# A filter's last layer and first DFT stage in parts of TensorE's array, and full end pieces in attention

## The chip, the cores and the metric

The kernel runs on one core of a Trainium2 chip. TensorE (PE in the profile) multiplies a stationary operand of up to 128x128 with a moving one and writes to PSUM; VectorE (DVE), ScalarE (ACT) and GpSimd (POOL) do the rest, SyncE (SP) issues the transfers. The metric is the device time of one execution in microseconds.

## The reference

An encoder layer is applied to two sequences, A (1024 tokens) and B (512 tokens), with the same weights. Two branches work on the same normalised input: a long convolution with a filter that a small network generates, and attention in three dilated groups. Gates, an output projection and an MLP follow. The parts that the change touches:

```python
def implicit_filter(L, w1, b1, w2, b2, w3, b3, freq, w_out):
    ...
    h = jnp.sin(fr * (h @ w3.astype(f32) + b3.astype(f32)))
    h = h @ w_out.astype(f32)
    ...
    decay = jnp.exp(-t * deltas[None, :])
    h_fwd, h_bwd = jnp.split(h, 2, axis=-1)
    h_fwd, h_bwd = h_fwd * decay, h_bwd * decay
    k2 = jnp.concatenate([h_fwd, jnp.zeros((1, D_HYENA), f32), h_bwd[1:][::-1]], axis=0)
    return k2 / jnp.sum(jnp.abs(k2), axis=0, keepdims=True)

def long_conv(u, k2, d):
    ...
    K = jnp.fft.rfft(k2, n=2 * L, axis=0)
    y = jnp.fft.irfft(U * K[None], n=2 * L, axis=1)[:, :L]
    return (y + uf * d.astype(jnp.float32)).astype(u.dtype)

def banded_attention(q, k, v, bias_vec, radius):
    ...
    p = jnp.exp(s - m)
    den = jnp.sum(p, axis=-1, keepdims=True)
    o = jnp.einsum('...bqk,...bkd->...bqd', p, vw.astype(jnp.float32)) / den
```

The filter has 64 hidden units and 768 channels, forward and backward; the radius of each attention group is 64 keys on each side (in the group's dilated order).

## The kernel before

**The main stream.** All large projections go through one helper, `mm3` (its matmul is L756). Weights and activations are split into a high and a low part, and three products are summed: 128x128 weights, 512 tokens moving. There are 9504 such matmuls. The units of work (18 for the convolution's inputs, 18 for queries, keys and values, 16 gates, the mixing, the output and the MLP, for A and then B) run in a fixed list; names like `zhyA__mm` or `qkvA__mm` tell the unit's kind and group.

**The side work.** Filters, convolutions, attention, norms and gates are generators that yield a cost and a latency at each step, in microseconds. While a unit emits its products, `pump` advances a clock by their cost and, in proportion, resumes side generators that are ready. So the costs that a generator yields set which side work is written between which products. ACT runs in the order in which the program is written; for PE, DVE, POOL and SP the framework's scheduler orders the instructions when the program is built, and each engine then works strictly through its list.

**The filter** (`filt_gen`, `filt_third`). Taps are handled in blocks of 128: 64 forward taps and 64 backward taps. A has 16 blocks, B has 8. The hidden layer's values for a block are a stationary 128x128 tile of `sall`, block-diagonal: 64 hidden units by 64 forward taps above, 64 by 64 backward taps below, zeros elsewhere, which a memset on POOL writes once. The channels are taken in thirds of 256. For each third and each group of four blocks (`jg`), `taps` multiplies that tile with the output weights `fwo` (L835, two blocks into one PSUM bank by `pss2`), DVE multiplies by the decay (L837), ACT takes absolute values (L840) and POOL adds them up (L841) for the norm, which L858 sums over partitions. `stage1` is the first DFT stage: the constant 128x128 tile `f1k` (in `csq`) times the taps (L848), copied out by ACT (L376, the helper `copy`) and stored. `f1k` has nonzero values only in two 64x64 quarters, from forward rows to one half of the outputs for two of the four `q`, and from the backward rows. `stage2` follows with 128x128 constants (L878).

Each step of `taps` and `stage1` handles two blocks and then yields 0.9. Small products take their PSUM from a ring of four banks (`pss`); the main stream has a ring of its own.

**Attention** (`att_gen`). A chain handles 128 queries (or two times 128): scores (L1216, 64 rows of the array for each of two heads, into two banks), scale and bias and maximum on DVE (L1222, L1225), exponentials on ACT (L1232), transposes of the probabilities (L1242), copies by ACT, and P·V (L1256), where the two head pairs write partitions 0 to 63 and 64 to 127. The window of keys is split at multiples of 128, so each chain has two pieces: in the middle both have 128 keys; at the ends, and in half of the windows of group 1, one has 64. Then transposes give 64 rows, a copy is made for each piece, and P·V takes 64 rows of the array for one piece and 128 for the other. Eight chains have such a piece (six in A, two in B).

Of the kernel before, what the change touches and what calls it, by code (L numbers as in the profile page):

```python
# [13 lines left out]
AF = mybir.ActivationFunctionType  # L14
# [47 lines left out]

def _filter_consts(L):
# [15 lines left out]

    decay = decay.reshape(J // 4, 4, 128, 3, 256).transpose(3, 0, 2, 1, 4)  # L80
# [3 lines left out]
def _dft_consts():  # L84
# [10 lines left out]
    f1k = np.zeros((2, 4, 16, 4, 32))  # L95
# [230 lines left out]
def _program(ctx, tc, d, outs):  # L326
# [435 lines left out]
    def filt_gen(S):  # L762
# [7 lines left out]
        sall = g((J // 2, 128)), g((J // 2, 128))  # L770
        for s in sall:
            G_.memset(s, 0.0)
# [24 lines left out]
        for ck in range(2):  # L797
            A.activation(sall[ck][0:64, :, 0:64], arg[64 * ck:64 * ck + 64].rearrange("p (j c) -> p j c", c=64), AF.Sin)
        yield 0.0, 1.0
        for j in range(J):  # L800
            dst = sall[j // nj][64:128, j % nj, 64:128]
# [13 lines left out]
    def filt_third(S, th, sall, fwo):  # L815
# [9 lines left out]
        def taps(jg):  # L825
# [4 lines left out]
            k2[jg] = kt  # L830
            for jp in range(2):
                ps = pss2()
                for jj in range(2):
                    j = 4 * jg + 2 * jp + jj
                    T.matmul(ps[:, jj], sall[j // (J // 2)][:, j % (J // 2), :], fwo[:, cs], start=True, stop=True)  # L835
                sl = slice(2 * jp, 2 * jp + 2)
                V.tensor_tensor(kt[:, sl], ps, dec[:, sl], ALU.mult)  # L837
# [3 lines left out]
                G_.tensor_tensor(acc, acc, ab, ALU.add)  # L841

        def stage1(jg):
            st = g((4, 256))
            for jp in range(2):
                ps = pss2()
                for jj in range(2):
                    T.matmul(ps[:, jj], f1k, k2[jg][:, 2 * jp + jj], start=True, stop=True)  # L848
                copy(st[:, 2 * jp:2 * jp + 2], ps)
                yield 0.9, 0.0  # L850
# [287 lines left out]
    def v_unit(S, gi, f, ratio):  # L1138
# [44 lines left out]
    def att_gen(S, gi):  # L1183
# [11 lines left out]
        def keys(i):  # L1195
# [6 lines left out]
            return k0, k1, [(t0 - k0, min(n, k1 - t0), vv) for t0, n, vv in vts if k0 <= t0 < k1]  # L1202


        def chain(tiles):
# [6 lines left out]
            s = [sp.tile([128, 512 // w, w], F32, tag="sc", name=nm("sc"), bufs=4) for _ in range(2)]  # L1212
            for a, f, i in slots:
# [22 lines left out]
            for hh in range(2):  # L1236
                pt = pss().rearrange("p (a b) -> p a b", a=4)
                pT.append(sp.tile([128, 4, 128], F32, tag="pT", name=nm("pT"), bufs=4))
                pieces = k[tiles[0]][2]
                for a, f, i in slots:  # L1240
                    for j, (o, n, _) in enumerate(k[i][2]):
                        T.transpose(pt[:n, a * np_ + j], s[hh][:, a, o:o + n], ident)  # L1242
                na = len(slots) * np_
                if all(n == 128 for _, n, _ in pieces):
                    copy(pT[hh][:, :na], pt[:, :na])
                else:
                    for j, (o, n, _) in enumerate(pieces):
                        copy(pT[hh][:n, j:na:np_], pt[:n, j:na:np_])
            yield 0.22 * np_ * len(slots), LPT
            po = pss().rearrange("p (a b) -> p a b", a=4)  # L1250
            for b, i in enumerate(tiles):
                for hh in range(2):
                    for j, (o, n, vv) in enumerate(k[i][2]):
                        for f in range(2):
                            h = 2 * f + hh
                            T.matmul(po[64 * f:64 * f + 64, 2 * b + hh], vv[:n, 64 * h:64 * h + 64],  # L1256
                                     pT[hh][:n, (2 * b + f) * np_ + j], start=j == 0, stop=j == np_ - 1)
# [471 lines left out]
```

## Time and profile before

| | |
|---|---|
| median of 3 runs | 2676.79 us (2670.54 to 2680.43) |
| profiled execution | 2664.77 us, its span 2663.0 us |
| PE busy | 2591.3 us (97%) |
| DVE, ACT, POOL busy | 1253.4, 863.9, 153.2 us |
| mean granted clock of TensorE | 0.990 |
| last layer and first DFT stage (L835, L848) | 288 instructions on PE |
| P·V of attention (L1256) | 448 instructions on PE, 64 of them on 64 rows |

In the groups of instructions a row names line, engine, operation, result and operands, then the rows and columns of the array that are used (128*32 is 128 rows and 32 columns), the moving operand (128x256) and the count; after the bar stand busy time, mean duration in ns, and idle time ahead with its cause. In a timeline a row gives start, duration, engine and the same names. A matmul's duration runs to the end of its pass through the array, and the next one starts before that; so what one costs is read from the distance of starts.

### The profile page before, as it was taken

The numbers are of one execution on the slowest core, as the hardware profiler recorded it, in microseconds if no ns is written. First come the engines' busy times: TensorE is split into PE (matmuls) and PEld (weight loads), VectorE is DVE, ScalarE is ACT, GpSimd is POOL, SyncE is SP. The second block draws the span as 40 slices with busy tenths as digits, with TensorE's granted clock in tenths as the row PEclk, the third lists the DMA queues.
The fourth block names the chain that finished last, engine by engine and source line by source line (L and its number), as shares of the span: only waits on it lengthen the run. The fifth ranks groups of instructions, "written<-read, shape, count | busy, mean of one in ns | idle before, by whom it ended". The sixth has DMA issues, their size and how long they took to land.

```text
span 2663.0 us, 30782 instructions
## 1 busy us (share of the span) xinstructions
PE 2591.3 (97%) x12296; PEld 2096.3 (79%) x12296; DVE 1253.4 (47%) x1626; ACT 863.9 (32%) x1414; POOL 153.2 (6%) x108
## 2 busy tenths in 40 slices
PE   8999999999899999999799999999999999999999
PEld 4778888687688777878578877888888888888887
DVE  5354444554658544554455464333333333554544
ACT  5443232533423444443333342112111221322332
POOL 0110100000001211000022210000000000000000
PEclk9999999999999999999899999999999999999999
DMA  7354455565756443446763532111111111422222
GB/s 270 126 165 158 155 165 174 154 187 143 220 204 227 145 135 96 150 153 220 223 202 130 189 126 69 50 48 48 48 48 55 49 43 54 149 101 91 102 95 103
DMA packets 138101, 350.98 MB, mean 132 GB/s; under 512 B 19016, under 2 KB 50303, under 8 KB 137830
## 3 DMA queue, kind: packets, MB, share of 16 engines
q1 hardware_dynamic: 137670, 348.22, 40.1%
q8 instruction: 97, 1.59, 0.3%
q0 software_dynamic: 288, 0.79, 0.1%
q14 instruction: 46, 0.38, 0.0%
HBM read 280.67 MB, written 71.16 MB: 132 GB/s over the span
## 4 chain that ended last, share of the span: by engine, by line
PE 86%; DVE 5%; DMA 4%; ACT 2%; issue 1%; SPq 1%; POOL 1%; DVEq 0%; ACTq 0%; POOLq 0%
PE ffA__mm L756 26%; PE ffB__mm L756 13%; PE zhyA__mm L756 7%; PE qkvA__mm L756 6%; PE mixA__mm L756 6%; PE gateA__mm L756 5%; PE zhyB__mm L756 4%; PE qkvB__mm L756 3%; PE mixB__mm L756 2%; PE gateB__mm L756 2%; PE convA__s L999 1%; DMA mixA__g<-zhyA__dr 1%; PE convA__s L974 1%; PE attA__s L1256 1%; PE filtA__s L878 1%
## 5 line engine op out<-in xcount | busy, mean ns | idle before, releaser
L756 PE MATMUL ffA__mm<-ffA__g,ffA__wh 128*128 128x512 f32 x1024 | 274.1, 389 | 0.0
L756 PE MATMUL ffA__mm<-normA__g,ffA__wh 128*128 128x512 f32 x992 | 265.1, 389 | 0.0
L756 PEld LDWEIGHTS ffA__mm<-ffA__g,ffA__wh 128*128 128x128 f32 x1024 | 192.0, 188 | 40.5 <-issue 0.4
L756 PEld LDWEIGHTS ffA__mm<-normA__g,ffA__wh 128*128 128x128 f32 x992 | 186.2, 188 | 38.7
L1507 DVE SCALAR_TENSOR_TENSOR mixA__g<-ffA__mm,adam,mixA__g 128x1024 f32<-128x1024 f32 x64 | 82.1, 1283 | 190.0 <-PE ffA__mm L756 190.0
L756 PE MATMUL ffB__mm<-ffB__g,ffB__wh 128*128 128x512 f32 x512 | 157.8, 389 | 0.0
L756 PE MATMUL ffA__mm<-ffA__g,ffA__wl 128*128 128x512 f32 x512 | 157.6, 389 | 0.0
L756 PE MATMUL zhyA__mm<-init__g,zhyA__wh 128*128 128x512 f32 x512 | 150.8, 410 | 3.1 <-DVE zhyA__g L1023 3.1
L756 PE MATMUL ffB__mm<-normB__g,ffB__wh 128*128 128x512 f32 x496 | 152.7, 389 | 0.0
L756 PE MATMUL ffA__mm<-normA__g,ffA__wl 128*128 128x512 f32 x496 | 152.7, 389 | 0.0
L389 ACT CAST ffA__wh<-ffA__wr 128x1024 fp32r<-128x1024 f32 x63 | 66.3, 1053 | 256.6 <-PE ffA__mm L756 213.6
L1489 DVE SCALAR_TENSOR_TENSOR ffA__g<-ffA__mm,ffA__g 128x1024 f32<-128x1024 f32 x32 | 39.2, 1225 | 222.4 <-ACT ffA__g L1488 222.4
L756 PE MATMUL gateA__mm<-init__g,gateA__wh 128*128 128x512 f32 x480 | 132.1, 394 | 5.1 <-ACT gateA__wh L389 5.1
L756 PE MATMUL qkvA__mm<-init__g,qkvA__wh 128*128 128x512 f32 x416 | 119.1, 402 | 0.0
L756 PE MATMUL mixA__mm<-mixA__g,mixA__wh 128*128 128x512 f32 x424 | 115.4, 392 | 3.7 <-DVE mixA__g L1441 2.0
L756 PEld LDWEIGHTS zhyA__mm<-init__g,zhyA__wh 128*128 128x128 f32 x512 | 94.4, 189 | 23.9 <-issue 6.4
L756 PEld LDWEIGHTS ffB__mm<-ffB__g,ffB__wh 128*128 128x128 f32 x512 | 96.0, 188 | 20.3 <-ACT ffB__g L389 0.2
L756 PEld LDWEIGHTS ffA__mm<-ffA__g,ffA__wl 128*128 128x128 f32 x512 | 96.1, 188 | 20.0
L1488 ACT ACTIVATE ffA__g<-ffA__mm 128x1024 f32<-128x1024 f32 x32 | 33.0, 1030 | 237.3 <-PE ffA__mm L756 237.3
L756 PEld LDWEIGHTS gateA__mm<-init__g,gateA__wh 128*128 128x128 f32 x480 | 90.0, 189 | 24.1 <-ACT gateA__wh L389 5.3
L756 PEld LDWEIGHTS ffB__mm<-normB__g,ffB__wh 128*128 128x128 f32 x496 | 93.1, 188 | 19.4
L756 PEld LDWEIGHTS ffA__mm<-normA__g,ffA__wl 128*128 128x128 f32 x496 | 93.1, 188 | 19.3
(495 smaller groups left out, 5013.4 us busy)
## 6 DMA issues: line engine op xcount, KB each, us to landing
ada__g<-ada SPq DMA_DIRECT2D x32, 512.0 KB, 4.3
ffA__wr<-w_up SPq DMA_DIRECT2D x32, 512.0 KB, 3.1
ffA__wr<-w_dn SPq DMA_DIRECT2D x32, 512.0 KB
ffB__wr<-w_dn SPq DMA_DIRECT2D x32, 512.0 KB
ffB__wr<-w_up SPq DMA_DIRECT2D x30, 512.0 KB, 3.2
filtA__dr<-filtA__g SPq DMA_DIRECT2D x24, 512.0 KB, 3.6
convA__g<-filtA__dr SPq DMA_DIRECT2D x48, 256.0 KB, 6.2
init__g<-ada SPq DMA_DIRECT2D x16, 512.0 KB, 10.5
```

What stands on the lines that cost most here:

```text
L389: A.copy(hi, raw)
L756: T.matmul(ps[:, 512 * c:512 * c + 512], ww[:, sl], xx(k)[:, 512 * c:512 * c + 512], start=k == 0 and p == 0, stop=k == kt - 1 and p == 2)
L878: T.matmul(ps[:, ee], cm[:, e], sin[:, e], start=True, stop=True)
L974: T.matmul(ps[:, ee], cb_[:, 2 * ep + ee], y[:, 2 * ep + ee], start=True, stop=True)
L999: T.matmul(ps[:, :, 4 * j8:4 * j8 + 4], bt[j // 4][:, j % 4, 128 * cc:128 * cc + 128], ibm, start=True, stop=True)
L1256: T.matmul(po[64 * f:64 * f + 64, 2 * b + hh], vv[:n, 64 * h:64 * h + 64], pT[hh][:n, (2 * b + f) * np_ + j], start=j == 0, stop=j == np_ - 1)
L1488: A.activation(r, ps[:, :L], AF.Relu)
L1489: V.scalar_tensor_tensor(r, ps[:, :L], 0.0, r, ALU.max, ALU.mult)
L1507: V.scalar_tensor_tensor(S.h(m), ps[:, :L], mod(S, 5, m), S.h(m), ALU.mult, ALU.add)
```

## The change

**Filter.** `sall` holds only the two 64x64 quarters, side by side as [128, 16 blocks, 64], so that no zeros are stored or multiplied. A block's product is four parts: 64 hidden units by 32 taps each, on 64 rows and 32 columns of the array. `TAPS` says which quarter of the taps goes to which 32 columns. It alternates the row halves along the columns and differs between the first and the second pair of blocks in a group, so that two blocks, one from each pair, use all eight 64x32 parts of the array, each block writing its own bank. The decay's rows are permuted in the same way. `f1k` becomes two 64x128 halves with a copy for either arrangement, and the DFT stage does two blocks at once in four 64x64 parts. Both steps now handle all four blocks of a group and yield 1.3 once, instead of 0.9 twice.

**Attention.** A piece of 64 keys is filled to 128: the missing rows of `vo` are set to zero, the scores' tile gets zero columns past the window (a memset on POOL for each tile of scores), transposes and P·V always have 128 rows, and one copy takes all pieces.

```diff
+TAPS = ((0, 3, 1, 2), (2, 1, 3, 0))
...
+    piece = decay.reshape(J, 4, 32, DH)
+    decay = np.stack([piece[j, list(TAPS[j % 4 // 2])] for j in range(J)]).reshape(J, 128, DH)
...
-            f1k[0, q, :, q, r] = col(p[:16], r)
-            f1k[1, 3 - q, :, q, r] = col(31 - p[:16], r)
+            if q < 2:
+                for h in range(2):
+                    for s in range(2):
+                        f1k[h, s, q, :, s, q, r] = col(p[:16], r)
+                        f1k[h, 1 - s, 1 - q, :, s, q, r] = col(31 - p[:16], r)
...
-        sall = g((J // 2, 128)), g((J // 2, 128))
-        for s in sall:
-            G_.memset(s, 0.0)
+        sall = g((J, 64))
+        G_.memset(sall[64:128, 0], 0.0)
...
+            ps = pss2(), pss2()
+            for jj in range(2):
+                for jp in range(2):
+                    for i, c in enumerate(TAPS[jp]):
+                        rs = slice(64 * (c // 2), 64 * (c // 2) + 64)
+                        T.matmul(ps[jp][32 * i:32 * i + 32, jj], sall[rs, 4 * jg + 2 * jp + jj, 32 * (c % 2):32 * (c % 2) + 32],
+                                 fwo[rs, cs], start=True, stop=True)
             for jp in range(2):
-                ps = pss2()
-                for jj in range(2):
-                    j = 4 * jg + 2 * jp + jj
-                    T.matmul(ps[:, jj], sall[j // (J // 2)][:, j % (J // 2), :], fwo[:, cs], start=True, stop=True)
                 sl = slice(2 * jp, 2 * jp + 2)
-                V.tensor_tensor(kt[:, sl], ps, dec[:, sl], ALU.mult)
-                yield 0.9, LTAP
+                V.tensor_tensor(kt[:, sl], ps[jp], dec[:, sl], ALU.mult)
+            yield 1.3, LTAP
...
             st = g((4, 256))
+            ps = pss2(), pss2()
+            for jj in range(2):
+                for jp in range(2):
+                    for h in range(2):
+                        o = 64 * (h ^ jp)
+                        T.matmul(ps[jp][o:o + 64, jj], f1k[64 * h:64 * h + 64, 64 * jp:64 * jp + 64],
+                                 k2[jg][64 * h:64 * h + 64, 2 * jp + jj], start=True, stop=True)
             for jp in range(2):
-                ps = pss2()
-                for jj in range(2):
-                    T.matmul(ps[:, jj], f1k, k2[jg][:, 2 * jp + jj], start=True, stop=True)
-                copy(st[:, 2 * jp:2 * jp + 2], ps)
-                yield 0.9, 0.0
+                copy(st[:, 2 * jp:2 * jp + 2], ps[jp])
+            yield 1.3, 0.0
...
+                            if n < 128:
+                                G_.memset(vo[n:, o + a_], 0.0)
...
+            pieces = k[tiles[0]][2]
+            full = max(o for o, _, _ in pieces) + 128
+            for t in s if full > nk else ():
+                G_.memset(t[:, :, nk:full], 0.0)
...
-                        T.transpose(pt[:n, a * np_ + j], s[hh][:, a, o:o + n], ident)
+                        T.transpose(pt[:, a * np_ + j], s[hh][:, a, o:o + 128], ident)
                 na = len(slots) * np_
-                if all(n == 128 for _, n, _ in pieces):
-                    copy(pT[hh][:, :na], pt[:, :na])
-                else:
-                    for j, (o, n, _) in enumerate(pieces):
-                        copy(pT[hh][:n, j:na:np_], pt[:n, j:na:np_])
+                copy(pT[hh][:, :na], pt[:, :na])
...
-                            T.matmul(po[64 * f:64 * f + 64, 2 * b + hh], vv[:n, 64 * h:64 * h + 64],
-                                     pT[hh][:n, (2 * b + f) * np_ + j], start=j == 0, stop=j == np_ - 1)
+                            T.matmul(po[64 * f:64 * f + 64, 2 * b + hh], vv[:, 64 * h:64 * h + 64],
+                                     pT[hh][:, (2 * b + f) * np_ + j], start=j == 0, stop=j == np_ - 1)
```

Since the steps yield other costs, side work stands at other places in the engines' lists, and since the lines shift, the changed kernel's numbers differ: `mm3` is L768, taps L848, the first DFT stage L867, the norm's sum L879, scores L1243, transposes L1268, P·V L1278. In the rows that follow, the number behind "x" at the end is a count, and the shape is that of the result in PSUM.

TensorE at the first group of taps of A's filter, before:

```order
L756 MATMUL qkvA__mm_750<-init__g_255,qkvA__wl_661 128x512 x2
L835 MATMUL filtA__s_764<-filtA__g_447,filtA__g_449 128x256 x2
L756 MATMUL qkvA__mm_750<-init__g_316,qkvA__wh_660 128x512 x2
L756 MATMUL qkvA__mm_750<-init__g_320,qkvA__wh_660 128x512 x2
L756 MATMUL qkvA__mm_750<-init__g_316,qkvA__wl_661 128x512 x2
L650 MATMUL qkvA__s_774<-qkvA__g_654,csq 32x256 x4
L650 MATMUL qkvA__s_774<-qkvA__g_740,csq 32x256 x4
L835 MATMUL filtA__s_789<-filtA__g_447,filtA__g_449 128x256 x2
```

and now:

```order
L848 MATMUL filtA__s_762<-filtA__g_447,filtA__g_449 32x256 x4
L848 MATMUL filtA__s_763<-filtA__g_447,filtA__g_449 32x256 x4
L848 MATMUL filtA__s_762<-filtA__g_447,filtA__g_449 32x256 x4
L848 MATMUL filtA__s_763<-filtA__g_447,filtA__g_449 32x256 x4
L662 MATMUL qkvA__s_782<-qkvA__g_652,csq 32x256 x4
L662 MATMUL qkvA__s_782<-qkvA__g_738,csq 32x256 x4
L768 MATMUL qkvA__mm_748<-init__g_316,qkvA__wh_658 128x512 x2
```

Two steps of two matmuls, with six products of the main stream between them, have become one step of 16, which writes two banks (762 and 763) in turn.

TensorE at the first DFT stage of A's last third, before:

```order
L848 MATMUL filtA__s_2300<-filtA__g_2272,csq 128x256 x2
L848 MATMUL filtA__s_2304<-filtA__g_2272,csq 128x256 x2
L858 MATMUL filtA__s_2309<-filtA__g_2070,csq 128x256 x2
L848 MATMUL filtA__s_2318<-filtA__g_2153,csq 128x256 x2
L848 MATMUL filtA__s_2322<-filtA__g_2153,csq 128x256 x2
L848 MATMUL filtA__s_2328<-filtA__g_2213,csq 128x256 x2
```

and now:

```order
L867 MATMUL filtA__s_2347<-filtA__g_2313,csq 64x256 x3
L867 MATMUL filtA__s_2348<-filtA__g_2313,csq 64x256 x2
L867 MATMUL filtA__s_2347<-filtA__g_2313,csq 64x256
L867 MATMUL filtA__s_2348<-filtA__g_2313,csq 64x256 x2
L879 MATMUL filtA__s_2360<-filtA__g_2105,csq 128x256 x2
L867 MATMUL filtA__s_2369<-filtA__g_2195,csq 64x256 x2
L867 MATMUL filtA__s_2370<-filtA__g_2195,csq 64x256 x2
L867 MATMUL filtA__s_2369<-filtA__g_2195,csq 64x256 x2
L867 MATMUL filtA__s_2370<-filtA__g_2195,csq 64x256 x2
```

The stage stands at the same place, with eight matmuls for a group of four blocks instead of four.

TensorE after an attention chain of A's group 0, with taps of the filter's second third, now:

```order
L1278 MATMUL attA__s_1379<-attA__pT_1341,qkvA__g_1133 64x128 x4
L848 MATMUL filtA__s_1391<-filtA__g_447,filtA__g_449 32x256 x4
L848 MATMUL filtA__s_1392<-filtA__g_447,filtA__g_449 32x256 x4
L848 MATMUL filtA__s_1391<-filtA__g_447,filtA__g_449 32x256 x4
L848 MATMUL filtA__s_1392<-filtA__g_447,filtA__g_449 32x256 x4
L1243 MATMUL attA__s_1411<-qkvA__g_840,qkvA__g_465 128x256
L1243 MATMUL attA__s_1412<-qkvA__g_840,qkvA__g_465 128x256
L1243 MATMUL attA__s_1411<-qkvA__g_853,qkvA__g_502 128x256
L1243 MATMUL attA__s_1412<-qkvA__g_853,qkvA__g_502 128x256
```

Here the taps' two banks are followed at once by scores into two more; before, six products of the main stream stood on each side of two of the taps' matmuls.

More of the change, by code (lines that the diff above doesn't have):

```diff
@@ L797, in filt_gen @@
         for ck in range(2):
[L798 removed]
+            A.activation(sall[0:64, nj * ck:nj * ck + nj],
+                         arg[64 * ck:64 * ck + 64].rearrange("p (j c) -> p j c", c=64), AF.Sin)
         yield 0.0, 1.0
         for j in range(J):
[L801 removed]
+            dst = sall[64:128, j]
             q0 = Q - 4 * j - 3
@@ L844, in stage1 @@
             st = g((4, 256))
-            for jp in range(2):
-                ps = pss2()
-                for jj in range(2):
-                    T.matmul(ps[:, jj], f1k, k2[jg][:, 2 * jp + jj], start=True, stop=True)
-                copy(st[:, 2 * jp:2 * jp + 2], ps)
-                yield 0.9, 0.0
+            ps = pss2(), pss2()
+            for jj in range(2):
+                for jp in range(2):
+                    for h in range(2):
+                        o = 64 * (h ^ jp)
+                        T.matmul(ps[jp][o:o + 64, jj], f1k[64 * h:64 * h + 64, 64 * jp:64 * jp + 64],
+                                 k2[jg][64 * h:64 * h + 64, 2 * jp + jj], start=True, stop=True)
+            for jp in range(2):
+                copy(st[:, 2 * jp:2 * jp + 2], ps[jp])
+            yield 1.3, 0.0
             del k2[jg]
@@ L1201, in keys @@
                 k1 = min(k0 + per, n0 + 192)
-            return k0, k1, [(t0 - k0, min(n, k1 - t0), vv) for t0, n, vv in vts if k0 <= t0 < k1]
+            return k0, k1, [(t0 - k0, n if n < 128 else min(n, k1 - t0), vv) for t0, n, vv in vts if k0 <= t0 < k1]
         def chain(tiles):
@@ L1238, in chain @@
                 pT.append(sp.tile([128, 4, 128], F32, tag="pT", name=nm("pT"), bufs=4))
-                pieces = k[tiles[0]][2]
                 for a, f, i in slots:
-                    for j, (o, n, _) in enumerate(k[i][2]):
-                        T.transpose(pt[:n, a * np_ + j], s[hh][:, a, o:o + n], ident)
+                    for j, (o, _, _) in enumerate(k[i][2]):
+                        T.transpose(pt[:, a * np_ + j], s[hh][:, a, o:o + 128], ident)
                 na = len(slots) * np_
-                if all(n == 128 for _, n, _ in pieces):
-                    copy(pT[hh][:, :na], pt[:, :na])
-                else:
-                    for j, (o, n, _) in enumerate(pieces):
-                        copy(pT[hh][:n, j:na:np_], pt[:n, j:na:np_])
+                copy(pT[hh][:, :na], pt[:, :na])
             yield 0.22 * np_ * len(slots), LPT
@@ L1252, in chain @@
                 for hh in range(2):
-                    for j, (o, n, vv) in enumerate(k[i][2]):
+                    for j, (_, _, vv) in enumerate(k[i][2]):
                         for f in range(2):
                             h = 2 * f + hh
-                            T.matmul(po[64 * f:64 * f + 64, 2 * b + hh], vv[:n, 64 * h:64 * h + 64],
-                                     pT[hh][:n, (2 * b + f) * np_ + j], start=j == 0, stop=j == np_ - 1)
+                            T.matmul(po[64 * f:64 * f + 64, 2 * b + hh], vv[:, 64 * h:64 * h + 64],
+                                     pT[hh][:, (2 * b + f) * np_ + j], start=j == 0, stop=j == np_ - 1)
             for b, i in enumerate(tiles):
```

3 lines of the change are left out of this document (2 added, 1 removed).

## The prediction

> **What bounds the kernel now.** I read the engines' busy times first, then the chain that ended last, then the stretches in which the filter runs.
>
> ```profile
> span 2663.0 us, 30782 instructions
> PE 2591.3 (97%) x12296; PEld 2096.3 (79%) x12296; DVE 1253.4 (47%) x1626; ACT 863.9 (32%) x1414; POOL 153.2 (6%) x108
> ...
> PE 86%; DVE 5%; DMA 4%; ACT 2%; issue 1%; SPq 1%; POOL 1%; DVEq 0%; ACTq 0%; POOLq 0%
> ```
>
> TensorE is busy for 97% of the span, and 86% of the chain is its work. But an average over stages does not say whether it binds where the change is made. Group A's filter and its first attention groups run from 84 to 310 us, group B's filter from 929 to 1200 us:
>
> ```profile
> 84.00:310.00 226.00, 224.43 (x1161) 182.13 (x1160) 101.08 (x140) 91.41 (x202) 33.20 (x26) 1.00 0.43 141
> 310.00:930.00 620.00, 595.90 (x3043) 482.02 (x3043) 341.82 (x549) 217.67 (x426) 28.54 (x22) 0.98 0.58 181
> 929.00:1200.00 271.00, 268.66 (x1408) 214.90 (x1407) 140.19 (x227) 125.92 (x281) 21.14 (x16) 1.00 0.42 133
> 1200.00:1330.00 130.00, 113.27 (x492) 91.33 (x491) 53.96 (x67) 40.97 (x55) 2.39 (x1) 0.93 0.69 220
> ```
>
> The columns after the stretch's length are the busy times of PE, its weight loads, DVE, ACT and POOL. In the two filter stretches PE lacks 1.6 of 226 us and 2.3 of 271 us, at a granted clock of 1.00. Side work there always finds a large product of the main stream beside it. So in these stretches a microsecond of PE work less should be a microsecond of time less. In the other two PE lacks 24.1 and 16.7 us: there it waits for transfers, and there the gain could be lost or enlarged.
>
> **The filter's products.** A program's fp32 matmul is two instructions in the profile, which I call passes.
>
> ```profile
> L835 PE MATMUL filtA__s<-filtA__g,filtA__g 128*128 128x256 f32 x96 | 24.6, 380 | 0.0
> L848 PE MATMUL filtA__s<-filtA__g,csq 128*128 128x256 f32 x96 | 22.7, 379 | 0.0
> L835 PE MATMUL filtB__s<-filtB__g,filtB__g 128*128 128x256 f32 x48 | 12.6, 380 | 0.0
> L848 PE MATMUL filtB__s<-filtB__g,csq 128*128 128x256 f32 x48 | 11.9, 381 | 0.0
> ```
>
> The 380 ns are one pass from its start to its end; passes overlap, so the price is the distance of starts, which the chain shows:
>
> ```profile
> 104.58 1.73 PE filtA__s L835 x8
> 302.06 5.18 PE filtA__s L848 x24
> 749.60 58.29 PE gateA__mm L756 x256
> ```
>
> 1.73/8 and 5.18/24 are both 0.216 us per pass of 256 columns; a pass of the main stream (512 columns) costs 58.29/256 = 0.228 us. Last layer (L835) and first DFT stage (L848) together are 288 passes, 62.2 us of PE. Per group of four blocks each is 8 passes, 1.73 us. There are 12 such groups for A (four times three thirds) and 6 for B.
>
> The change turns the 8 passes of the last layer into 32 (16 matmuls of 64x32), those of the stage into 16 (8 of 64x64). Whether that is cheaper depends only on how many run at once. The trace has the case of four column strips, twice, and that of two row halves:
>
> ```profile
> 94.49 0.62 PE L756 MATMUL qkvA__mm<-init__g,qkvA__wl 128*128 128x512 f32 x2
> 95.04 1.07 PE L650 MATMUL qkvA__s<-qkvA__g,csq 128*32 128x256 f32 x16
> 96.04 1.13 PE L835 MATMUL filtA__s<-filtA__g,filtA__g 128*128 128x256 f32 x4
> ...
> 901.38 0.64 PE L1071 MATMUL qkvB__s<-qkvB__g,csq 128*32 128x128 f32 x16
> 901.95 0.66 PE L1320 MATMUL combineA__s<-csq,combineA__g 128*128 128x128 f32 x4
> ...
> 716.20 1.16 PE L1216 MATMUL attA__s<-qkvA__g,qkvA__g 64*128 64x128 f32 x16
> 717.29 0.50 PE L756 MATMUL gateA__mm<-init__g,gateA__wl 128*128 128x512 f32 x1
> 717.63 0.39 PE L756 MATMUL gateA__mm<-init__g,gateA__wh 128*128 128x512 f32 x1
> ```
>
> L650's 16 passes take 96.04 - 95.04 = 1.00 us. One after the other they would take 16 x 0.216 = 3.46 us, four at a time 0.86 us, so four do run at once. L1071 puts 16 passes into 0.57 us, 36 ns each with their weight loads, so issuing eight in 0.216 us (27 ns each) is near what has been done. L1216 puts 16 passes of two row halves into 1.09 us, where a pass of 128 columns takes half of 0.216: two at a time.
>
> So I take eight 64x32 parts, or four 64x64 parts, per 0.216 us. A group of four blocks is then four rounds in both stages, 0.86 instead of 1.73 us. Saved: 18 groups x 2 stages x 0.865 = **31.1 us**. No row has eight at once. The bound from below is four at once, L650's number: the last layer then needs eight rounds, 1.73 us as before, and half of the 31.1 us, 15.6 us, is gone. From above nothing is faster than the passes of one strip, so 31.1 us is the most.
>
> **Going in and out.** Between the two main-stream passes at 94.49 us and L650 lie 0.55 us instead of 2 x 0.228: 0.10 us. L650's 1.00 us hold 0.14 us beyond the four rounds. The first full pass after such a visit takes 717.63 - 717.29 = 0.34 instead of 0.228 us: 0.11 us. So a visit costs 0.35 us, 0.175 us for each change of array shape. In TensorE's order I count 142 changes of shape before and 186 after (those inside attention's P·V left out, which come next): the 36 stage groups make 33 visits, while side work that now stands together saves some. 44 x 0.175 = **7.7 us lost**; with L1216's visit (0.22 beyond its eight rounds, the same 0.10 and 0.11) 9.5 us, with L650's inner and following parts alone (0.25 us a visit) 5.5 us.
>
> **Attention's end pieces.** P·V of a chain with an end piece, and of one without:
>
> ```profile
> 160.45 1.54 PE L1256 MATMUL attA__s<-attA__pT,qkvA__g 64*64 64x128 f32 x16
> 161.92 1.09 PE L1242 MATMUL attA__s<-csq,attA__sc 128*128 128x128 f32 x8
> ...
> 179.31 1.09 PE L1256 MATMUL attA__s<-attA__pT,qkvA__g 128*64 128x128 f32 x16
> 180.33 1.09 PE L1242 MATMUL attA__s<-csq,attA__sc 128*128 128x128 f32 x8
> ```
>
> The same 16 passes take 1.47 us where 64-row and 128-row pieces alternate and 1.02 us where they do not. Full pieces take 0.45 us off each of 8 such chains (two ends and four half windows in A, two ends in B): **3.6 us gained**, at most this and at least nothing. The transposes keep their number. The fills are 12 memsets of 128x2x64 and 4 of 64x256 on POOL, 6% busy, while the two large ones for the filter shrink. Some stand ahead of the filter's sums in POOL's queue, and PE's L858 waits for those sums; but these memsets wait only for transposes that stand earlier in PE's order than the taps whose sums are behind them.
>
> ```profile
> L819 POOL MEMSET filtA__g<- 128x512 f32 x3 | 1.6, 525 | 85.7 <-DMA filtA__dr<-filtA__g 34.9 <-DVE zhyA__g L1028 26.1 <-PE bias__s L1354 24.7
> ```
>
> Uncovered, 16 at 0.53 us (the time of a larger one) would be 8 us; I take 0, since POOL is idle.
>
> **New waits.** A group of taps now holds two of the four small PSUM banks until DVE has multiplied both, and both become ready together:
>
> ```profile
> L837 DVE TENSOR_TENSOR filtA__g<-filtA__s,filtA__g x24: 679/690/692, 94.3 to 297.3; 128x512 f32<-128x512 f32 x24
> L376 ACT COPY filtA__g<-filtA__s x24: 587/587/590, 125.8 to 307.3; 128x512 f32<-128x512 f32 x24
> ...
> PE filtA__s L858 <- POOL filtA__g L841: 1.4, 1, 1.4
> ```
>
> Where scores or transposes follow taps at once (at three places in the order), they want two banks more, or four, and wait up to 2 x 0.69 = 1.4 us. Where three stage groups stand in a row (at two places), PE needs 0.86 us a group and ACT 2 x 0.587 = 1.17 us, where before PE's 1.73 us hid the copies: the third group waits 2 x (1.17 - 0.86) = 0.6 us. The wait of L858 (1.4 us) stays. Queued behind each wait is the main stream, as PE works in order. Together up to 5.4 us; I take **4 us lost**, between 0 and 9, since other groups stand only a few passes from such work.
>
> **Sum:** -31.1 + 7.7 - 3.6 + 4 = -23.0 us. The profiled execution took 2664.8 us (span 2663.0), which becomes 2641.8. The runs shown have the median 2676.8, 12 us above it; the same difference gives **2654 us**.
>
> **Rivals.** *Four parts at once in the last layer.* For it speaks that no row shows more; against it, L1071's 36 ns per pass. Gain 15.6 us less: 2669 us.
>
> *The gain is given back later.* PE's idle 24.1 and 16.7 us come from convolution stages that wait for transfers. The filter now ends some 100 main-stream passes earlier in the order (740 against 846 before its last product), so convolutions start beside other units. I give this 8 us in either direction, a fifth of the 41 us of idle time. With the largest waits and dearest visits (-31.1 + 9.5 - 3.6 + 9 + 8) it leaves -8 us: 2669 us.
>
> *Slower: two row halves cannot write one bank together.* L1216's two halves write two banks, and L650's four strips write one bank from the same rows; in the change each block's bank gets strips from both halves. If a part must wait for the other half's part in its bank, and all behind it wait too, the parts go one by one: per group 32 x 0.216 = 6.91 instead of 1.73 us in the last layer and 16 x 0.216 = 3.46 in the stage, 18 x (5.18 + 1.73) = 124 us lost, with the other terms +133 us: 2809 us. If the halves only swap banks between rounds, both stages cost what they did, and the other terms give +8 us: 2685 us. It decides from the point where fewer than four 64x32 or two 64x64 parts run at once. Against it: strips lie on different partitions of the bank.
>
> The Trainium skill has a rule of this kind ("TensorEngine Tiling (Array Packing)", Restrictions and Gotchas): row tiles write to different PSUM banks and cannot use the same one at a time. No run here shows it yet; by it one of the last two times would hold. Against it stands "TensorE: Matmul & The Clock Gate", Part 3, with 16 tiles of 32x32 measured at 10.6 times one, by which my sum stays; it lays each row on its own bank, and the trace shows no more than four.
>
> **How the numbers follow.** The forecast 0.66; four at once 0.08; gain given back 0.10; banks 0.12 (of that 0.05 one by one); 0.04 for anything else. The forecast's own range is 2640 (cheap visits, no waits, 8 us gained later: -37.2) to 2669 us. With part of the bank rival I take 2638 to 2680 us. About 0.5%, 13.4 us, is what a measurement of this kernel tells from no change. Faster by more: nearly all of the forecast and a quarter of the two middling rivals, 0.68. Slower: one by one, some of the rest, 0.10. Within: 0.22.
>
> **What would show it.** Right: the filter's stages at about 0.86 us per group plus 0.35 us per visit in the timeline of PE; P·V of end chains at 1.02 us; the stretch up to the filter's end shorter by some 15 us for A and 8 for B; PE's idle time about 4 us longer there. Wrong: groups of taps at 1.73 us (four at once, or swapped banks) or 7 us (one by one), or short groups with PE idle longer by the same amount beyond 310 us.

## The result, and the profile after

| | before | after |
|---|---|---|
| median of 5 runs each, compared | 2676.79 us (2668.58 to 2681.09) | 2627.52 us (2624.71 to 2631.51) |
| profiled execution | 2664.77 us, span 2663.0 us | 2630.32 us, span 2628.5 us |
| ratio | | 0.9838 (95% interval 0.9819 to 0.9857) |

The change is 1.6% faster, 38 to 48 us by the interval. The prediction was 2654 us with a range from 2638 us: the sign was right, the size was not, and the time lies below the range.

Of the page after, the span and the busy times:

```profile
span 2628.5 us, 31915 instructions
PE 2562.4 (97%) x12872; PEld 2061.4 (78%) x12872; DVE 1248.1 (47%) x1626; ACT 860.8 (33%) x1398; POOL 152.0 (6%) x122
```

PE was without work for 2663.0 - 2591.3 = 71.7 us before and for 66.1 us now. The prediction had made PE wait longer, not shorter. The same four stretches as in the prediction (columns: PE, weight loads, DVE, ACT, POOL, granted clock, share of DMA, GB/s):

```profile
84.00:310.00 226.00, 221.35 (x1595) 169.34 (x1595) 106.70 (x149) 90.61 (x201) 33.24 (x32) 1.00 0.52 167
310.00:930.00 620.00, 601.00 (x3185) 486.99 (x3185) 349.25 (x558) 232.56 (x445) 35.58 (x34) 0.98 0.57 176
929.00:1200.00 271.00, 271.00 (x1589) 214.76 (x1589) 142.81 (x235) 118.77 (x260) 14.92 (x13) 1.00 0.51 161
1200.00:1330.00 130.00, 113.97 (x491) 92.37 (x491) 55.77 (x68) 44.01 (x59) 7.19 (x3) 0.91 0.68 214
```

In A's filter (84 to 310 us) PE now lacks 4.7 us where it lacked 1.6: new waits of the filter are there, 3.1 us. Elsewhere it lacks less: 19.0 for 24.1 us, 0.0 for 2.3 us (B's filter), 16.0 for 16.7 us. The 4 us of the forecast were for both filters, which together lack less than 1 us more.

The filter's products themselves, first in PE's timeline at the first group of taps (start, duration, then as before):

```profile
93.13 0.61 PE L768 MATMUL qkvA__mm<-init__g,qkvA__wl 128*128 128x512 f32 x2
93.67 1.09 PE L848 MATMUL filtA__s<-filtA__g,filtA__g 64*32 64x256 f32 x32
94.69 1.07 PE L662 MATMUL qkvA__s<-qkvA__g,csq 128*32 128x256 f32 x16
95.70 0.50 PE L768 MATMUL qkvA__mm<-init__g,qkvA__wh 128*128 128x512 f32 x1
...
122.72 1.13 PE L879 MATMUL filtA__s<-filtA__g,csq 128*128 128x256 f32 x4 [1.60 <-POOL filtA__g L858]
123.79 1.94 PE L867 MATMUL filtA__s<-filtA__g,csq 64*64 64x256 f32 x22
125.97 1.94 PE L867 MATMUL filtA__s<-filtA__g,csq 64*64 64x256 f32 x26 [0.25 <-DVE filtA__g L883]
127.84 0.50 PE L768 MATMUL qkvA__mm<-init__g,qkvA__wh 128*128 128x512 f32 x1
...
161.32 1.97 PE L1278 MATMUL attA__s<-attA__pT,qkvA__g 128*64 128x128 f32 x32
163.22 1.09 PE L848 MATMUL filtA__s<-filtA__g,filtA__g 64*32 64x256 f32 x32
164.24 1.13 PE L1243 MATMUL attA__s<-qkvA__g,qkvA__g 64*128 64x256 f32 x8
```

32 passes of taps take 94.69 - 93.67 = 1.02 us with what it costs to change shape, so eight parts do run at once: in the trace of the single passes eight start within 46 ns, the next eight from 240 ns on, and the 32 starts span 0.72 us. The 16 passes of a single stage group, four parts at once, take 1.02 us as well (the one from 193.4 us on). Two chains of P·V take 163.22 - 161.32 = 1.90 us, 0.95 each. Where three stage groups stand in a row, they take 127.84 - 123.79 = 4.05 us for 3 x 0.86 = 2.59 us of passes.

The waits of PE, longest in total first (total us, times, longest), of before:

```profile
PE init__s L698 <- ACT init__g L696: 9.3, 8, 7.1
PE convB__s L963 <- DMA convB__g<-convB__dr: 8.4, 2, 7.5
PE gateA__mm L756 <- ACT gateA__wh L389: 5.1, 1, 5.1
...
PE zhyA__mm L756 <- DVE zhyA__g L1023: 3.1, 1, 3.1
```

and after:

```profile
PE init__s L710 <- ACT init__g L708: 10.1, 8, 7.6
PE convB__s L1020 <- DMA convB__g<-convB__dr: 8.8, 1, 8.8
PE gateA__mm L768 <- ACT gateA__wh L401: 7.5, 1, 7.5
...
PE filtA__s L879 <- POOL filtA__g L858: 3.5, 3, 1.7
```

No single wait carries the gain: the three largest have grown, the norm's sum (L879) has grown from 1.4 to 3.5 us, and one of before (`zhyA__mm` for L1023) is gone, which comes up again below.

**Where the time went.** I took the starts of all PE passes from 25 us on and sorted what lies between successive starts: passes at their full rate (by the distances of the prediction: 0.216 us for 256 columns, a quarter of it each where four run at once, an eighth for eight); what is beyond that at a change of array shape, up to 0.24 us each; what is beyond it elsewhere (waits); and all of the excess, waits or slow passes, that lies in a stretch where the granted clock is one half. The last 376 us, an unbroken main stream alike in all kernels, are left out. The last two rows are kernels of the experiments below.

| us, one profiled execution each | passes | changes of shape | waits | excess at half clock | (time at half clock) |
|---|---|---|---|---|---|
| before | 2124.5 | 31.0 | 46.4 | 60.3 | 51 |
| before, profiled again | 2124.5 | 30.8 | 45.5 | 72.2 | 75 |
| the change | 2093.5 | 38.5 | 38.8 | 56.7 | 51 |
| whole products in the change's steps | 2124.5 | 22.1 | 33.7 | 54.8 | 48 |
| the change, yield 2.3 | 2093.5 | 48.3 | 45.9 | 75.4 | 85 |

Between the two profiles that is -31.0 us for passes, +7.5 for shapes, -7.6 for waits, -3.6 at half clock. The sorting is not firm in every column. The column of passes is a count at the prediction's prices. In three rows the excess at half clock is more than the time at half clock, so it holds waits from outside these stretches; if only gaps that touch such a stretch are counted, it goes from 40.3 us before to 44.3 us, and waits go from 65.1 to 51.1 us. The sum of the two is firm: 106.7 to 95.5 us by the table, 105.4 to 95.4 us by the other count.

When the two kernels are compared by the start of the same main-stream product, they are level at product 1152 (432 us), although A's filter, over by then in both, has 24 x 0.865 = 20.8 us of passes less. Of the convolution 6.1 us of passes have moved ahead of that point; the other 14.7 us are eaten by more excess, by the second count 5.2 us at changes of shape and 9.5 us in waits. From there to product 1536, in A's convolution, the passes cost the same (143.3 and 142.8 us), yet the change needs 154.5 us where before needs 173.8. So the gain shows at product 1536 (18.5 us), and then at 1920 (24.4 us) and 4224 (35.8 us).

### The profile page after: what moved, and what is told of

It reads as the page before. It is cut to its first block, busy times and chain, and to the rows that moved or that the text cites. A ratio compares the mean times of both kernels' runs of the same rounds, so it can differ in the third digit from the quotient of the medians.

```text
span 2628.5 us, 31915 instructions
## 1 busy us (share of the span) xinstructions
PE 2562.4 (97%) x12872; PEld 2061.4 (78%) x12872; DVE 1248.1 (47%) x1626; ACT 860.8 (33%) x1398; POOL 152.0 (6%) x122
## 4 chain that ended last, share of the span: by engine, by line
PE 50%; DVE 1%; DMA 1%; ACT 0%; issue 0%; SPq 0%; DVEq 0%; ACTq 0%
PE ffA__mm L768 27%; PE ffB__mm L768 13%; PE mixA__mm L768 6%; PE mixB__mm L768 2%; PE convB__s L1020 0%; DMA mixA__g<-zhyA__dr 0%; PE gateB__mm L768 0%; DVE mixB__wl L402 0%; ACT mixB__wh L401 0%; PE convB__s L995 0%; DVE mixA__g L402 0%; PE convB__s L984 0%; DMA convB__g<-convB__dr 0%; DVE normA__g L735 0%; DVE mixB__g L1491 0%
## 5 line engine op out<-in xcount | busy, mean ns | idle before, releaser
L768 PE MATMUL ffA__mm<-ffA__g,ffA__wh 128*128 128x512 f32 x1024 | 274.1, 389 | 0.0
L768 PE MATMUL ffA__mm<-normA__g,ffA__wh 128*128 128x512 f32 x992 | 265.1, 389 | 0.0
L768 PEld LDWEIGHTS ffA__mm<-ffA__g,ffA__wh 128*128 128x128 f32 x1024 | 192.0, 188 | 40.4 <-issue 0.4
L768 PEld LDWEIGHTS ffA__mm<-normA__g,ffA__wh 128*128 128x128 f32 x992 | 186.2, 188 | 38.6
L768 PE MATMUL ffB__mm<-ffB__g,ffB__wh 128*128 128x512 f32 x512 | 157.8, 389 | 0.0
L768 PE MATMUL ffA__mm<-ffA__g,ffA__wl 128*128 128x512 f32 x512 | 157.7, 389 | 0.0
L768 PE MATMUL ffB__mm<-normB__g,ffB__wh 128*128 128x512 f32 x496 | 152.7, 389 | 0.0
L768 PE MATMUL ffA__mm<-normA__g,ffA__wl 128*128 128x512 f32 x496 | 152.7, 389 | 0.0
L768 PE MATMUL zhyA__mm<-init__g,zhyA__wh 128*128 128x512 f32 x512 | 145.2, 400 | 0.0
L768 PE MATMUL gateA__mm<-init__g,gateA__wh 128*128 128x512 f32 x480 | 133.4, 398 | 7.5 <-ACT gateA__wh L401 7.5
L768 PE MATMUL mixA__mm<-mixA__g,mixA__wh 128*128 128x512 f32 x424 | 115.3, 392 | 3.1 <-DVE mixA__g L1463 1.9
L768 PE MATMUL qkvA__mm<-init__g,qkvA__wh 128*128 128x512 f32 x416 | 116.9, 399 | 0.0
L768 PEld LDWEIGHTS zhyA__mm<-init__g,zhyA__wh 128*128 128x128 f32 x512 | 94.2, 188 | 23.6 <-issue 5.7
L768 PEld LDWEIGHTS ffB__mm<-ffB__g,ffB__wh 128*128 128x128 f32 x512 | 96.0, 188 | 20.3 <-ACT ffB__g L401 0.2
L768 PEld LDWEIGHTS gateA__mm<-init__g,gateA__wh 128*128 128x128 f32 x480 | 90.5, 191 | 27.2 <-ACT gateA__wh L401 7.9
L768 PEld LDWEIGHTS ffA__mm<-ffA__g,ffA__wl 128*128 128x128 f32 x512 | 96.1, 188 | 20.0
L768 PEld LDWEIGHTS ffB__mm<-normB__g,ffB__wh 128*128 128x128 f32 x496 | 93.1, 188 | 19.4
L768 PEld LDWEIGHTS ffA__mm<-normA__g,ffA__wl 128*128 128x128 f32 x496 | 93.1, 188 | 19.3
```

Of the source, the lines that this page charges most:

```text
L768: T.matmul(ps[:, 512 * c:512 * c + 512], ww[:, sl], xx(k)[:, 512 * c:512 * c + 512], start=k == 0 and p == 0, stop=k == kt - 1 and p == 2)
```

## Experiments

Each ratio is to the kernel before on the same chip, with its 95% interval. A per cent is 26.7 us. Before's medians there were 2671.26, 2671.51 and 2670.88 us.

**The filter's part alone**: the change with attention as before.

```diff
-                copy(pT[hh][:, :na], pt[:, :na])
+                if all(n == 128 for _, n, _ in pieces):
+                    copy(pT[hh][:, :na], pt[:, :na])
+                else:
+                    for j, (o, n, _) in enumerate(pieces):
+                        copy(pT[hh][:n, j:na:np_], pt[:n, j:na:np_])
...
-                            T.matmul(po[64 * f:64 * f + 64, 2 * b + hh], vv[:, 64 * h:64 * h + 64],
-                                     pT[hh][:, (2 * b + f) * np_ + j], start=j == 0, stop=j == np_ - 1)
+                            T.matmul(po[64 * f:64 * f + 64, 2 * b + hh], vv[:n, 64 * h:64 * h + 64],
+                                     pT[hh][:n, (2 * b + f) * np_ + j], start=j == 0, stop=j == np_ - 1)
```

> The change without its attention part (pieces of 64 keys stay as they were); the filter's parts and steps as changed. The change gained about 43 us by the comparison of runs. If attention's full pieces are worth what they take off P.V (0.45 us for each of 8 chains, 3.6 us), this kernel loses about 4 us of the gain: about 39 us faster than before. Rival: the unexpected part of the gain (some 20 us) comes from attention, whose lines lost 17 us on TensorE between the traces: then this kernel is only 22 to 27 us faster than before.

Measured: 2631.62 us, 0.9840 (0.9821 to 0.9859). Within the intervals all of the change's gain is the filter's.

**The attention's part alone**: before with the full end pieces, the same lines the other way round.

> The kernel before with the attention part of the change alone. By the 3.6 us of P.V: 2 to 6 us faster than before, within the noise of the comparison. Rival (the unexpected gain is attention's): 15 to 20 us faster.

Measured: 2668.67 us, 0.9982 (0.9968 to 0.9995): 5 us faster, between 1 and 9. On top of the filter's part it adds 0.9840 - 0.9838 = 0.0002, nothing that can be told. Taken alone it agrees with the 3.6 us forecast; whether it adds to the filter's part is within the noise.

**Whole products in the change's steps**: steps of four blocks, two banks, yield 1.3 and full end pieces as in the change, but each block one 128x128 product with its zeros, as before. Only the parts of the array are undone; in the traces the side work on TensorE stands at the same main-stream products as in the change, to within two.

```diff
-                    for i, c in enumerate(TAPS[jp]):
-                        rs = slice(64 * (c // 2), 64 * (c // 2) + 64)
-                        T.matmul(ps[jp][32 * i:32 * i + 32, jj], sall[rs, 4 * jg + 2 * jp + jj, 32 * (c % 2):32 * (c % 2) + 32],
-                                 fwo[rs, cs], start=True, stop=True)
+                    j = 4 * jg + 2 * jp + jj
+                    T.matmul(ps[jp][:, jj], sall[j // (J // 2)][:, j % (J // 2), :], fwo[:, cs], start=True, stop=True)
...
-                    for h in range(2):
-                        o = 64 * (h ^ jp)
-                        T.matmul(ps[jp][o:o + 64, jj], f1k[64 * h:64 * h + 64, 64 * jp:64 * jp + 64],
-                                 k2[jg][64 * h:64 * h + 64, 2 * jp + jj], start=True, stop=True)
+                    T.matmul(ps[jp][:, jj], f1k, k2[jg][:, 2 * jp + jj], start=True, stop=True)
```

> The change with its steps (four blocks per step, cost 1.3, two banks at once) and its attention part, but with the old full 128x128 products for the last layer and the first DFT stage. So the order of the side work is about that of the change and only the array's parts are missing. Theory: the parts are worth 31.1 us of passes less 33 visits of 0.35 us, about 20 us, and what the forecast missed (some 20 us) is idle time that the new order removes: then this kernel is about 20 us slower than the change, 20 to 25 us faster than before. Rival: the order is worth nothing and the parts are worth more than their passes: then it stands within 5 us of before (attention's 3.6 us).

Measured: 2641.14 us, 0.9878 (0.9859 to 0.9897). Its first group of taps in PE's timeline:

```profile
92.86 1.89 PE L835 MATMUL filtA__s<-filtA__g,filtA__g 128*128 128x256 f32 x8
94.67 1.07 PE L650 MATMUL qkvA__s<-qkvA__g,csq 128*32 128x256 f32 x16
```

The group takes 1.81 us, where the change's takes 1.02. So no pass is saved here, and yet some 33 us of the 43 are there: against before, the table has 18.2 us less for waits and half clock and 8.9 us less for changes of shape. From product 1152 to 1536 this kernel needs 154.2 us, as the change does. The parts themselves are worth 0.9878 - 0.9838 = 0.0040, 11 us (4 to 18, with the two intervals taken as independent), though they save 31.0 us of passes: against these steps the table has +16.4 us for more changes of shape and +7.0 us for waits and half clock.

**The change at other paces.** Four kernels whose PE work is the change's, to the last pass; only the two yields differ, and with them the place of side work. The first has the rate of before, 1.8 for four blocks:

```diff
-            yield 1.3, LTAP
+            yield 1.8, LTAP
...
-            yield 1.3, 0.0
+            yield 1.8, 0.0
```

> The change with the costs that the two steps yield set back to their old sum (1.8 instead of 1.3 for four blocks), so that side work is written between the main stream's products at the old pace; the products are those of the change. Theory (the new pace, by which the filter ends about 100 main-stream products earlier, removes idle time): 8 to 16 us slower than the change, 27 to 35 us faster than before. Rival (the pace does not matter): the same as the change, about 43 us faster than before.

The others are the same lines with 0.9, 1.55 and 2.3:

> The change with the cost that the filter's two steps yield for four blocks set to 0.9 instead of 1.3; products and steps as changed. Theory (the order of the side work is a draw: which waits and half-clock stretches it leaves does not follow the pace): within -5 to +20 us of the change, in no line with 1.3 and 1.8. Rival (a faster pace is better as such, 1.8 lost about 9 us): 4 to 9 us faster than the change.

> The change with the pace 1.55. Theory (a draw): anywhere within -5 to +20 us of the change. Rival (time follows the pace): halfway between the change and the pace 1.8, 4 to 5 us slower than the change.

> The change with the pace 2.3, the one that made the old steps 17 us faster when they were slowed. Theory (a draw): within -5 to +20 us of the change. Rival (time follows the pace, 9 us for 0.5): about 18 us slower than the change.

| yield of a step | 0.9 | 1.3 (the change) | 1.55 | 1.8 | 2.3 |
|---|---|---|---|---|---|
| us | 2641.44 | 2627.52 | 2632.77 | 2639.79 | 2667.16 |
| ratio | 0.9884 | 0.9838 | 0.9853 | 0.9871 | 0.9984 |
| interval | 0.9865 to 0.9903 | 0.9819 to 0.9857 | 0.9834 to 0.9871 | 0.9851 to 0.9891 | 0.9973 to 0.9996 |

With the same products the time moves by 40 us. At 2.3 the whole gain of the change but 4 us is lost, twice the loss that was expected at most. The best of the five is 1.3, near the 1.2 us that such a group does take (0.86 and a visit's 0.35); at 1.55 the interval overlaps with it. That the optimum lies there because the clock of `pump` then fits is plausible, but five points that also differ by chance in what they collide with don't show it.

**Before at other paces**: the steps and products of before, with 0.65 and 1.15 instead of 0.9 for two blocks.

```diff
-                yield 0.9, LTAP
+                yield 0.65, LTAP
...
-                yield 0.9, 0.0
+                yield 0.65, 0.0
```

> The kernel before with nothing but the pace of the change: the two steps of the filter yield 0.65 instead of 0.9 (1.3 for four blocks). Products, steps and attention are those of before. The old pace cost the changed kernel about 9 us. Theory (the pace as such lets the filter end earlier and removes idle time): 6 to 12 us faster than before. Rival (the old order is only a poor draw, and any shift of the side work gains): 10 to 25 us faster, and the slowed pace in the next run gains as well.

> The kernel before with the pace moved the other way: the two steps of the filter yield 1.15 instead of 0.9. Theory (an earlier end of the filter removes idle time, a later one adds it): 5 to 10 us slower than before. Rival (the old order is a poor draw and any shift gains): 10 to 25 us faster than before.

Measured: at 0.65, which is the change's pace, 2679.25 us, 1.0029 (1.0017 to 1.0042); at 1.15 2652.42 us, 0.9936 (0.9917 to 0.9955). So the change's pace does not make before faster: it costs 8 us there, and a slower pace gains 17, while in the change a slower pace loses. The time hangs on the order that comes out, not on a direction of the pace.

**Grouping alone**: before with four blocks a step, two banks at once and one yield of 1.8, which is its old rate; whole products, attention as before.

```diff
+            ps = pss2(), pss2()
+            for jj in range(2):
+                for jp in range(2):
+                    j = 4 * jg + 2 * jp + jj
+                    T.matmul(ps[jp][:, jj], sall[j // (J // 2)][:, j % (J // 2), :], fwo[:, cs], start=True, stop=True)
             for jp in range(2):
-                ps = pss2()
-                for jj in range(2):
...
+            yield 1.8, LTAP
```

> The kernel before with nothing but the grouping: both steps of the filter handle four blocks at once with the old 128x128 products and yield 1.8 once instead of 0.9 twice; attention as before. If the parts of the change add up (array parts 10, pace 9, attention 5 of 43 us), the grouping alone is 15 to 22 us faster than before. Rival (the parts do not add up; grouping gains only with the new pace): within 5 us of before.

Measured: 2660.74 us, 0.9963 (0.9949 to 0.9977). Grouping is worth 10 us, pace costs 8, attention is worth 5, together 7; all three at once gained 33. So these pieces can't be added.

In the traces the side work of this kernel stands on TensorE, to within two main-stream products, where it stands in the change at 1.8. So those two differ in the products alone: 0.9963 - 0.9871 = 0.0092, some 25 us (18 to 31, reckoned in the same way) for the parts and the full end pieces together. Between the steps of 1.3 it was 11 us for the parts. What the parts are worth depends on the order in which they stand.

**One pair of blocks after the other**: the change, with the parts of the first pair of blocks (half of the array) all issued before those of the second pair, in both steps.

```diff
-            for jj in range(2):
-                for jp in range(2):
+            for jp in range(2):
+                for jj in range(2):
```

> The change with the loops over the two pairs of blocks exchanged, so that the parts of one pair (both blocks in one bank, four 64x32 parts or two 64x64 parts of the array) are issued before the parts of the other pair. Theory (TensorE takes parts in the order in which they are issued, so only half the array works): a group of four blocks needs 8 rounds, 1.73 us, in either step, and the kernel loses what the parts gained, about 15 us of passes; 10 to 20 us slower than the change. Rival (TensorE looks far enough ahead to start the other pair's parts): groups stay at 0.86 us and the time is the change's.

Measured: 2626.41 us, 0.9834 (0.9816 to 0.9853), the change's time. PE's timeline at its first group:

```profile
92.49 1.12 PE L848 MATMUL filtA__s<-filtA__g,filtA__g 64*32 64x256 f32 x32
93.54 1.07 PE L662 MATMUL qkvA__s<-qkvA__g,csq 128*32 128x256 f32 x16
```

1.05 instead of 1.02 us. The built order is really eight parts to one bank and then eight to the other; yet the single passes start in fours, 0, 54, 240 and 294 ns after the first, so passes for the second bank overtake those for the first that still wait for their part. The interleaving written by hand isn't needed.

**Before, profiled once more**, unchanged.

> The kernel before once more, for a second profile. Its first profiled execution took 2664.8 us, less than nearly all its timed runs (median 2671.5). Theory: the difference is in waits for transfers and in the stretches at half clock that follow them, so this profile shows more of both if it takes longer, and the same TensorE order and passes. Rival: the passes themselves vary.

Measured: 2675.60 us, span 2673.8 us. The clock (columns as in the stretches above) from 430 to 480 us, first in the profile shown so far, then in the new one:

```profile
430.00:480.00 50.00, 48.88 (x279) 41.98 (x277) 20.94 (x33) 12.20 (x19) 0.00 (x0) 1.00 0.55 179
```

```profile
430.00:480.00 50.00, 48.40 (x228) 41.94 (x228) 18.25 (x29) 7.82 (x11) 0.00 (x0) 0.83 0.51 168
```

In the same 50 us PE starts 279 passes in one execution and 228 in the other, busy both times: 17% of the clock is missing. Of the 10.8 us between the two spans 9.5 us are lost between 432 and 615 us, in A's convolution, by the starts of the same main-stream products. The 54 executions of before that were timed beside the experiments took 2663 to 2680 us, and this goes with the mean clock: six with 0.985 took 2677.1 us on average, five with 0.990 took 2666.3. The profile that the prediction was worked out from has 0.990. The change's five runs all have 0.990 to 0.992.

## Why the prediction was wrong

**Passes, right.** -31.1 us forecast. The table's -31.0 us is the count of passes at the same prices, so it is no second measurement; what bears it out are the groups of 1.02 us in both stages. Eight 64x32 and four 64x64 parts run at once; the rival of four at once is out.

**Row halves in one bank, right.** Strips of both halves write one bank at the same time, and the group takes 1.02 us, not 1.73 or 6.9. The Trainium skill's rule ("TensorEngine Tiling (Array Packing)", Restrictions and Gotchas), that row tiles cannot use the same bank at one time, does not hold here. The two write different partitions of the bank, and nothing was lost.

**Changes of shape and end pieces, nearly.** +7.7 - 3.6 = +4.1 us forecast, +7.5 us between the profiles by the table (+3.6 us if only the first start after a change is counted), both terms in one since an end piece is a change of shape too. P·V of an end chain takes 0.95 to 1.02 us as forecast. The count against before hides something, however. Before's end pieces alternate between shapes, in their transposes too, and without them all changes of shape from 25 us on fall from 242 to 196, while the time lost at them grows. Beside the same steps with whole products the parts pay 16.4 us for shapes (10.8 us by the narrower count), a third to a half of the passes that they save.

**New waits, the step that failed.** The prediction took 4 us lost (0 to 9) for waits, and gave the shift of later side work 8 us in either direction as a rival of 0.10. In A's filter the 3.1 us more of idle time come near to it, but by luck. At the three places where scores or transposes follow taps (from 164.24, shown above, 173.46 and 180.33 us), which were to cost up to 3 x 1.4 of the 5.4 us, PE does not wait at all. Instead the wait for the norm's sum, forecast to stay, grew by 2.1 us, and three stage groups take 1.5 us more than their passes, a visit's 0.35 us included. What failed is the step that counted waits in the filter alone and took the shift of later work for a small rival: the same change rewrites the order of everything that follows, and over the whole kernel waits and half clock fell by 7.6 + 3.6 us, so that the term is -11.2 us, not +4. That is 15 us of the 26.5 us by which the prediction missed. The runs put the size of this term at tens of us: 40 us among five kernels with equal products, 18 of the 33 us of the steps without any pass saved, 25 us between two paces of before. So the term is as large as the arithmetic.

**From the profile to the median, also failed.** "The same difference" of 12 us was added to the changed kernel. It is not a constant: most executions of before have more half-clock time than its profile had, as the second profile and the mean clocks show, and the five runs compared took longer than most (beside the experiments before's median is 2671 us, 6.5 us above the profile). The changed kernel's median lies 2.8 us below its own profile. That is the other 15 us of the miss; the shapes' 3.4 us stand against the two, and the rest is under 1 us.

**The tests named.** Groups at 0.86 us plus a visit, and P·V at 1.02 us: seen. Filter stretches shorter by 15 and 8 us: not seen; A's filter ends earlier, but up to product 1152 no time is gained. More idle time of PE in the filters: seen in A's, not in B's.

**What is open.** Which feature of the order makes it good. One marker separates the profiles: a unit of the convolution's inputs (`zhyA__mm`) that waits 2.1 to 3.2 us for DVE to empty PSUM (L1023 before, L1044 after). It is there in both profiles of before, in attention alone, in before at 0.65 and in the change at 2.3, whose medians are 2667 us or more, and in none of the other nine, all at 2661 or less. The time between the starts of main-stream products 1152 and 1536, the stretch of A's convolution in which it lies, separates them as well: 173.8 to 183.4 us in the five, 153.2 to 158.2 us in the nine. In before the wait looks like this, in DVE's timeline and then in PE's:

```profile
493.14 1.07 DVE L1222 SCALAR_TENSOR_TENSOR attA__sc<-attA__s,qkvA__rq,attA__g 128x192 f32<-128x192 f32 x3 [9.61 <-ACT zhyA__wh L389]
...
497.90 1.28 DVE L1023 SCALAR_TENSOR_TENSOR zhyA__g<-zhyA__mm,prm,zhyA__g 128x1023 f32<-128x1023 f32 x1
```

```profile
499.33 1.62 PE L756 MATMUL zhyA__mm<-init__g,zhyA__wh 128*128 128x512 f32 x3 [3.15 <-DVE zhyA__g L1023]
500.74 3.42 PE L963 MATMUL convA__s<-convA__g,convA__cm 128*128 128x256 f32 x8
503.80 0.59 PE L756 MATMUL zhyA__mm<-init__g,zhyA__wh 128*128 128x512 f32 x1
```

DVE idles 9.6 us ahead of an instruction of attention and empties the unit only at 497.90 + 1.28 = 499.18 us. PE stands 3.15 us, and then runs at half clock (eight passes in 503.80 - 500.74 = 3.06 us, where 8 x 0.216 = 1.73 is the full rate). Wait and half clock are some 5 us, so it marks the worse orders; by itself it makes up neither the 15 us or more of that stretch nor what lies between these kernels and the change. Moving that one chain was not tried.

## What to carry to other kernels

Parts of the array that are mostly zero are worth packing, but count the going in and out against the same steps with whole products: here 31 us of passes left 11 us in one order of the side work, and some 25 us, with the end pieces, in another. Where a cost model places side work, re-tune its costs after any change to the work, and try both directions, since identical instructions in another order differ by as much as the edit. Before a profile is carried over to a median, compare its granted clock with that of the timed runs.

## What the runs showed of the hardware

**Half clock outlasts a wait.** Before at 0.65 has the longest such stretch. Its clock, and PE's timeline in it:

```profile
705.00:714.00 9.00, 2.94 (x8) 1.24 (x8) 6.94 (x20) 4.82 (x19) 0.00 (x0) 0.60 0.74 231
714.00:745.00 31.00, 30.94 (x124) 26.44 (x125) 9.86 (x21) 8.02 (x27) 0.00 (x0) 0.51 0.38 136
745.00:760.00 15.00, 15.00 (x101) 11.56 (x100) 10.62 (x23) 9.82 (x43) 0.00 (x0) 1.00 0.53 179
```

```profile
714.06 0.79 PE L756 MATMUL gateA__mm<-init__g,gateA__wh 128*128 128x512 f32 x1 [5.66 <-ACT gateA__wh L389]
...
726.86 13.91 PE L999 MATMUL convA__s<-csq,convA__g 128*128 128x64 f32 x64
740.53 1.20 PE L756 MATMUL gateA__mm<-init__g,gateA__wh 128*128 128x512 f32 x2
```

A wait of 5.66 us, and then 31 us of work without a gap at half clock: 0.214 us a pass of L999 (13.67 us for 64). In before the same line takes 4.66 us for 42 passes, 0.111 us each:

```profile
728.77 4.85 PE L999 MATMUL convA__s<-csq,convA__g 128*128 128x64 f32 x42
733.43 1.18 PE L756 MATMUL gateA__mm<-init__g,gateA__wh 128*128 128x512 f32 x4
```

In the profiles of before, of the change, of before at 0.65 and of the change at 2.3 such stretches last 3.4, 6.8, 10.2, 13.7, 17.1 or 37.5 us, multiples of 3.4. The Trainium skill ("TensorE: Matmul & The Clock Gate", Part 1) gives a window of about 3.4 us and the half clock, and has full clock back after at least one busy window. The lengths agree; that one busy window is enough does not show here, where some nine (31 / 3.4) went by. What the clock counts as busy no run here shows. Nor is the wait shown as the one cause: a mean clock of 0.60 over the first 9 us means some 7.2 us at one half, so the clock fell near 706.8 us, and this wait began only at 714.06 - 5.66 = 708.40 us. By an estimate the wait and the work at half clock cost 5.7 + 31/2, some 21 us.

**Parts overtake each other.** Passes for free parts of the array start ahead of earlier ones whose part is taken (the kernel with one pair of blocks after the other, above: starts in fours at 0, 54, 240 and 294 ns). So what is said ahead of the prediction, that each engine works strictly through its list, does not hold for TensorE between the parts of its array.
